# Moving the projection of gate tile 0's first branch from the gate stage into the last attention unit

## Chip, cores and metric

The kernel runs on one NeuronCore (core 0) of a Trainium2 chip. The metric is the device time of one execution in microseconds. Before the change the median of three runs is 918.4 us (917.24 to 919.42). All work is in 32-bit floats; a matmul in full precision is made of three passes over operands split in a high and a low part.

## What is computed

One decoder block on `x` of 1024 positions by 1024 channels. What matters here, cut from the reference:

```
h = rms_norm(x, g_pre)
proj = einsum('bsd,dn->bsn', h, w_in)
qa, ka, va, fa, za, qb, kb, vb, zb, gates = split(proj)
ya = fox_attention(qa, ka, va, log_sigmoid(fa + b_forget)) * silu(za)
yb = rms_norm(diff_attention(rope(qb), rope(kb), vb)) * silu(zb)
gate_a, gate_b = split(sigmoid(gates), 2)          # 1024 channels each
merged = gate_a * (ya @ w_branch[0]) + gate_b * (yb @ w_branch[1])
out = x + rms_norm(merged @ w_out, g_post)
```

The gates are thus a projection of `h` by 2048 columns of `w_in` (from column `GT` = 4104) followed by a sigmoid. They depend on nothing that the attention computes.

## The kernel before, in words

Everything is kept channel-major: a tile is 128 channels by 1024 positions, worked in two chunks `c` of 512 positions. `hT[part][kh][sh]` holds the normalised input, part 0 the high and part 1 the low part; all eight tiles stay in SBUF until the gate stage ends.

Stages in order:

1. Normalise and transpose `x`, project the values (L197), and write combinations of `h` to DRAM (`t_d`, four of them, 2 MB each).
2. Attention: eight units `u` (0 to 3 differential, 4 to 7 forgetting). A unit's work is a list of `groups`; a group is two blocks of 128 query rows: `row` makes logits on TensorE (L432, L433; `s_row`), VectorE adds the bias and takes the maximum (L434), ScalarE the exponential (L440), VectorE the reciprocal (L557), GpSimd the scaling (L558). Then `av` transposes the weights (L461), splits them on ScalarE and VectorE (L464, L465), multiplies by the values (L485) and evacuates (L567, L568), and SyncE stores them (L571). A group's `av` is traced after the rows of the next group (`pend`).
3. Between groups stand projections that depend on no attention result, as work to fill TensorE: the next unit's q and k, the z tiles (`z_tasks`, through `spill_tasks`: `load_w`, `project` at L278, copy at L373, store to DRAM at L374) and sums of squares. In unit 7 the list `fill` holds only the four chunks of z tiles 6 and 7, placed after its groups 0, 1, 2 and 4 (counted from 0). Unit 7 has eight groups, from the longest rows to the shortest; the last two have rows of at most 256 positions.
4. The gate stage. `h_load` (L818) reads the `t_d` combinations back into eight tiles `T`, 1 MB each, in the SBUF that attention used. `gates_plain(0)` projects gate tile 0 directly: for branch 0 and 1 a weight load (`load_w`: DMA at L260, high part on ScalarE at L264, low part on GpSimd at L268) and two chunks of 24 matmuls (L278), each followed by a sigmoid from PSUM and a store to `g_d` (L797, L798). Gate tiles 1 to 7 go through `gates_pair`, which makes a 2x2 block product in seven products `m` of 12 matmuls (L735): the weight combinations on GpSimd (L699), their split (L686, L687), sums on VectorE (L728), sigmoid and store by `gate_out`. Products 1, 2 and 3 read `hT`; 4, 5, 6 and 7 read `T`. For tiles 1 to 6 the order is `GATE` = (1, 2, 4, 6, 5, 7, 3).
5. `y_load` (L782) and `y_work` bring the attention results back beside the gate products; then the branch products (L869), `merge`, and the output product with its norm.

What sets the order: the program is traced by Python loops, and a planner orders each engine's instructions by simulated time; among the instructions that are ready it takes the one traced first. On the chip each engine then runs its own list in order. All DMAs here (but one) are issued by SyncE in its list's order, and an issue that has to wait holds those behind it. Weights share pool slots: two each of `wraw` (raw), `whi` and `wlo`; the split left operands `a_g` of `gates_pair` rotate over `whi`, `wlo` and a third pair, `wop`. `pj` is a PSUM pool of two banks for the fill projections; `tmp` has ten 128x512 tiles for gates and z.

The context `tc.issue_after(ins)` makes the matmuls traced in it stand behind `ins` in TensorE's list; it adds no wait.

Of the kernel before, what the change touches and what calls it, by code (L numbers as in the profile page):

```python
# [9 lines left out]
F32 = mybir.dt.float32  # L10
# [6 lines left out]
P = 128  # L17
S = 1024
D = 1024
KT = D // P  # L20
NB = S // P
CH = 512
# [8 lines left out]
FING = (0,)  # L31
YORD = ((), ((4, 0), (4, 1)), ((5, 0), (5, 1), (6, 0)), ((6, 1), (7, 0), (7, 1)),
        ((0, 0), (0, 1), (1, 0)), ((1, 1), (2, 0), (2, 1)), ((3, 0), (3, 1)), ())
ZFILL = ((0,), (1,), (), (2,), (3,), (4,), (5,), (6, 7))
BIG = 3.0e38
EPS = 1e-6
# [3 lines left out]
QA, KA_, VA, ZA, QB, KB_, VB, ZB, GT = 0, 512, 1024, 1544, 2056, 2568, 3080, 3592, 4104  # L40
# [7 lines left out]
def tile_hybrid_block(  # L48
# [18 lines left out]
    nc = tc.nc  # L67
# [37 lines left out]
    cum_d = dram.tile([8, S], F32, name="cum_d")  # L105
    y_d = [dram.tile([P, S], F32, name=f"y_d{t}") for t in range(8)]
    g_d = [[dram.tile([P, S], F32, name=f"g_d{d}_{b}") for b in range(2)] for d in range(KT)]
    ss_d = dram.tile([4, S], F32, name="ss_d")
    rs_d = dram.tile([4, S], F32, name="rs_d")
    z_d = [dram.tile([P, S], F32, name=f"z_d{t}") for t in range(8)]  # L110
# [172 lines left out]
    with ExitStack() as st:  # L283
# [19 lines left out]
        def unit_proj(u):  # L303

            diff = u < 4
            t = u if diff else u - 4
            qc, kc = (QB, KB_) if diff else (QA, KA_)
            T = {}
            for n in ("TA", "TB", "KA", "KB"):
                T[n] = qk.tile([P, S], F32R, tag=n, name=f"{n}{u}")  # L310

            def rope(ps, c, nm):
                sl = slice(c * CH, (c + 1) * CH)
                raw = stg.tile([P, CH], F32, tag="raw", name=f"raw{nm}", bufs=4)
                nc.scalar.copy(raw, ps)
                sw = stg.tile([P, CH], F32, tag="sw", name=f"sw{nm}")
                for b in range(4):
                    o = b ^ 1
                    nc.sync.dma_start(sw[b * 32:(b + 1) * 32, :], raw[o * 32:(o + 1) * 32, :])
                rot = stg.tile([P, CH], F32, tag="raw", name=f"rot{nm}", bufs=4)  # L320
                nc.vector.tensor_tensor(rot, ps, cosT[:, sl], op=ALU.mult)
                nc.gpsimd.tensor_tensor(sw, sw, sinT[:, sl], op=ALU.mult)
                nc.vector.tensor_tensor(rot, rot, sw, op=ALU.add)
                return rot

            def stack(A, B, src, sl):

                nc.scalar.copy(A[UPR, sl], src[UPR])
                nc.vector.tensor_tensor(A[DNR, sl], src[UPR], A[UPR, sl], op=ALU.subtract)
                nc.scalar.copy(B[DNR, sl], src[DNR])  # L330
                nc.vector.tensor_tensor(B[UPR, sl], src[DNR], B[DNR, sl], op=ALU.subtract)  # L331

            def q_chunk(wt, c):
                sl = slice(c * CH, (c + 1) * CH)
                ps = pj.tile([P, CH], F32, tag="pj", name=f"pq{u}_{c}")
                project(ps, wt, c)
                src = rope(ps, c, f"q{u}_{c}") if diff else ps
                stack(T["TA"], T["TB"], src, sl)

            def k_chunk(wt, c):  # L340
                sl = slice(c * CH, (c + 1) * CH)
                ps = pj.tile([P, CH], F32, tag="pj", name=f"pk{u}_{c}")
                project(ps, wt, c)
                src = rope(ps, c, f"k{u}_{c}") if diff else ps
                stack(T["KA"], T["KB"], src, sl)

            box = {}

            def mk(kind, c, c0):
                def run():  # L350
                    if kind not in box:
                        box[kind] = load_w(f"{kind}{u}", w_cols(c0))
                    (q_chunk if kind == "q" else k_chunk)(box[kind], c)
                return run

            tasks = [mk("k", 0, kc + t * P), mk("q", 0, qc + t * P),
                     mk("k", 1, kc + t * P), mk("q", 1, qc + t * P)]
            return T, tasks
# [57 lines left out]
                    vload.pop(0)()  # L416
            return t

        lastx, vload = [None], []

        def s_row(T, m, i, X, bias, boff, nm, le=None):

            A, B = (T["TA"], T["KA"]) if m == 0 else (T["TB"], T["KB"])
            n = (i + 1) * P
            qs = slice(i * P, (i + 1) * P)
            xs = slice(i % 2 * P, (i % 2 + 1) * P)
            pr = pp.tile([P, S], F32, tag="P", name=f"P{nm}_{m}_{i}")
            mx = small.tile([P, 2], F32, tag="mx", name=f"mx{nm}_{m}_{i}", bufs=8)
            pcs = pieces(i)
            for j, (a, b) in enumerate(pcs):  # L430
                ps = sps.tile([P, CH], F32, tag="S", name=f"S{nm}_{m}_{i}_{j}")[:, 0:b - a]
                nc.tensor.matmul(ps, lhsT=A[:, qs], rhs=B[:, a:b], start=True, stop=False)  # L432
                nc.tensor.matmul(ps, lhsT=X[:, xs], rhs=B[:, a:b], start=False, stop=True)  # L433
                nc.vector.tensor_tensor_reduce(  # L434
                    out=pr[:, a:b], in0=ps, in1=bias[:, boff + a:boff + b], scale=-0.125,
                    scalar=BIG if j == 0 else mx[:, j - 1:j], op0=ALU.add, op1=ALU.min,
                    accum_out=mx[:, j:j + 1])
            if le is None:
                le = small.tile([P, 1], F32, tag="l", name=f"l{nm}_{m}_{i}", bufs=8)
            nc.scalar.activation(pr[:, 0:n], pr[:, 0:n], AF.Exp,  # L440
                                 bias=mx[:, len(pcs) - 1:len(pcs)], scale=-1.0, accum_out=le)
            return pr, le
# [156 lines left out]
        def forget_sums():  # L599
# [27 lines left out]
            nc.vector.tensor_scalar(cum, cum, -8.0, None, op0=ALU.mult)  # L627
            nc.sync.dma_start(cum_d, cum)

        T, tasks = unit_proj(0)  # L630
        for tk in tasks:
            tk()
# [2 lines left out]
        for u in range(8):  # L635
            load, load_v, groups = nxt or unit_attn(u, T)
            nxt = None
            if u == 0:
                vload.append(load_v)
            if u == 1:  # L640
                forget_sums()
            load()
            fill = []
            if u + 1 < 8:
                T, tasks = unit_proj(u + 1)
                fill += tasks
            for t in ZFILL[u]:
                fill += z_tasks(t)
            for t in SFILL[u]:
                fill += [lambda t=t, c=c: sum_squares(t, c) for c in range(2)]  # L650
                fill.append(lambda t=t: subln_scales(t))
            total = sum(s[0] for s in groups)
            done, nf = 0, 0
            for n, (wgt, rws, prd) in enumerate(groups):
                if n == len(groups) // 2 and u < 7:
                    nxt = unit_attn(u + 1, T)
                    vload.append(nxt[1])
                for r in rws:
                    r()
                if pend:  # L660
                    pend()
                pend = prd
                done += wgt
                while nf < len(fill) and nf < len(fill) * done / total:
                    fill[nf]()
                    nf += 1
        pend()

    bigs.close()
# [126 lines left out]
    def gate_out(d, br, c, g, src):  # L796
        nc.scalar.activation(g, src, AF.Sigmoid)  # L797
        nc.sync.dma_start(g_d[d][br][:, c * CH:(c + 1) * CH], g)  # L798

    def gates_plain(d):  # L800
        for br in range(2):
            wt = load_w(f"g{br}_{d}", w_cols(GT + br * D + d * P), True, True)
            for c in range(2):
                ps = xps.tile([P, CH], F32, tag="x", name=f"pg{d}_{br}_{c}")
                project(ps, wt, c)
                gate_out(d, br, c, tmp.tile([P, CH], F32, tag="t", name=f"g{d}_{br}_{c}"), ps)
# [14 lines left out]
    def gates_pair(d, order):  # L821
        raw = []
        for br in range(2):
            r = wpool.tile([P, KT, P], F32, tag="wraw", name=f"raw{d}_{br}")
            nc.sync.dma_start(r, w_cols(GT + br * D + d * P))
            raw.append(r)
        left = left_operands(f"g{d}", raw[0][:, 0:4], raw[0][:, 4:8], raw[1][:, 0:4], raw[1][:, 4:8])
        run_all(wino(f"g{d}", left, h_ops, order,
                     *(lambda t, br=br, c=c: gate_out(d, br, c, t, t)
                       for br in range(2) for c in range(2))))  # L830
# [2 lines left out]
    GATE = (1, 2, 4, 6, 5, 7, 3)  # L833
    h_load()
    gates_plain(0)
    for t in (4, 5, 6, 7, 0, 1, 2, 3):
        y_load(t)
    for d in range(1, KT):
        gates_pair(d, GATE if d < KT - 1 else (7, 5, 6, 4, 1, 2, 3))
        for t, c in YORD[d]:  # L840
            y_work(t, c)
    tst.close()
# [218 lines left out]
```

## Time and profile before

| | us |
|---|---|
| median of three runs | 918.4 |
| the profiled execution | 922.06 |
| its span, first to last instruction | 920.2 |
| TensorE busy | 887.9 (96%) |
| VectorE busy | 606.7 (66%) |
| GpSimd busy | 469.7 (51%) |
| ScalarE busy | 440.4 (48%) |
| gate stage: first matmul of `gates_plain(0)` | 585.39 |

How to read it: times in the views count from the first instruction's start. PE is TensorE's matmul, PEld its weight load, DVE VectorE, ACT ScalarE, POOL GpSimd, SP SyncE. Matmuls are pipelined, so the duration of one (0.39 us for 512 columns) is longer than the distance between the starts of two. A row of windows has for each engine the busy us with the number of instructions in brackets, then the granted clock, the share of the DMA engines and GB/s. A bracket at the end of a timeline row, such as [0.72 <-DVE plf L465], is the idle time before it and what ended it.

### The profile page before, as it was taken

The numbers are of one execution on the slowest core, as the hardware profiler recorded it, in microseconds if no ns is written. First come the engines' busy times: TensorE is split into PE (matmuls) and PEld (weight loads), VectorE is DVE, ScalarE is ACT, GpSimd is POOL, SyncE is SP. The second block draws the span as 40 slices with busy tenths as digits, with TensorE's granted clock in tenths as the row PEclk, the third lists the DMA queues.
The fourth block names the chain that finished last, engine by engine and source line by source line (L and its number), as shares of the span: only waits on it lengthen the run. The fifth ranks groups of instructions, "written<-read, shape, count | busy, mean of one in ns | idle before, by whom it ended". The sixth has DMA issues, their size and how long they took to land. (4 is left out here: it accounts for less than half of the span.)

```text
span 920.2 us, 13659 instructions
## 1 busy us (share of the span) xinstructions
PE 887.9 (96%) x4600; PEld 747.4 (81%) x4600; DVE 606.7 (66%) x1123; ACT 440.4 (48%) x877; POOL 469.7 (51%) x439
## 2 busy tenths in 40 slices
PE   7999999899999999999999999999999999999995
PEld 5899978788887888888888887788888878887874
DVE  6756546878668664467648547416778783549896
ACT  3433225566657675365546648524443461313442
POOL 7325324545545456254434446317676436787851
PEclk9999999999999999999999999999999999999998
DMA  9556737434336350432523331596555497300352
GB/s 315 188 176 256 259 90 197 123 79 123 107 77 172 75 178 18 138 92 72 167 69 97 117 109 54 220 399 207 172 176 169 154 342 258 88 28 25 101 173 91
DMA packets 121416, 136.95 MB, mean 149 GB/s; under 512 B 10225, under 2 KB 88049, under 8 KB 120322
## 3 DMA queue, kind: packets, MB, share of 16 engines
q1 hardware_dynamic: 121202, 135.82, 47.0%
q8 instruction: 36, 0.59, 0.3%
q14 instruction: 34, 0.28, 0.1%
q10 hardware_dynamic: 144, 0.26, 0.1%
HBM read 85.65 MB, written 37.81 MB: 134 GB/s over the span
## 5 line engine op out<-in xcount | busy, mean ns | idle before, releaser
L197 PE MATMUL pv<-wvhi,hT 128*128 128x264 f32 (+2 forms) x384 | 88.9, 324 | 0.4 <-DVE hT L183 0.4
L278 PE MATMUL pz<-hT,hi_z 128*128 128x512 f32 x256 | 83.3, 397 | 0.2 <-ACT sq L390 0.2
L278 PE MATMUL pk<-hT,hi_k 128*128 128x512 f32 x256 | 82.3, 395 | 0.9 <-DVE KB L331 0.9
L278 PE MATMUL pq<-hT,hi_q 128*128 128x512 f32 x256 | 82.9, 399 | 0.0
L735 PE MATMUL x_o<-wo_op,a_o 128*128 128x512 f32 x336 | 78.3, 393 | 1.6 <-ACT a_o L686 1.1
L869 PE MATMUL pb<-yT,hi_br 128*128 128x512 f32 x256 | 78.4, 389 | 0.0
L735 PE MATMUL x_g<-T,a_g 128*128 128x512 f32 x336 | 78.1, 391 | 0.0
L735 PEld LDWEIGHTS x_o<-wo_op,a_o 128*128 128x128 f32 x336 | 62.8, 188 | 17.0 <-ACT a_o L686 2.0
L735 PEld LDWEIGHTS x_g<-T,a_g 128*128 128x128 f32 x336 | 63.1, 188 | 13.9
L197 PEld LDWEIGHTS pv<-wvhi,hT 128*128 128x128 f32 x384 | 64.3, 190 | 6.1 <-DVE hT L183 0.7
L440 ACT ACTIVATE Pd<-Pd,mxd 128x128 f32<-128x128 f32 (+7 forms) x64 | 49.6, 775 | 35.4 <-DVE mxd L434 35.1
L553 POOL TENSOR_TENSOR cb<-cb,trim 128x128 f32<-128x128 f32 x64 | 30.1, 475 | 65.9 <-DVE mxf L434 44.7
L527 POOL TENSOR_SCALAR Pd<-Pd,l,nlam 128x128 f32<-128x128 f32 (+7 forms) x32 | 29.2, 912 | 67.0 <-DVE l L526 60.7
L197 PE MATMUL pv<-wvlo,hT 128*128 128x512 f32 (+2 forms) x192 | 61.9, 325 | 0.4 <-DVE wvlo L153 0.4
L558 POOL TENSOR_SCALAR Pf<-Pf,lf 128x1024 f32<-128x1024 f32 (+3 forms) x64 | 47.7, 750 | 27.7 <-DVE lf L557 24.6
L465 DVE TENSOR_TENSOR plf<-ptf,phf 128x512 fp32r<-128x512 f32 (+1 forms) x80 | 50.0, 635 | 18.0 <-ACT phf L464 17.1
L440 ACT ACTIVATE Pf<-Pf,mxf 128x1024 f32<-128x1024 f32 (+3 forms) x64 | 49.8, 778 | 20.6 <-DVE mxf L434 19.9
L735 PE MATMUL x_g<-hT,a_g 128*128 128x512 f32 x252 | 59.0, 391 | 0.0
L869 PEld LDWEIGHTS pb<-yT,hi_br 128*128 128x128 f32 x256 | 48.1, 188 | 9.9
L278 PEld LDWEIGHTS pq<-hT,hi_q 128*128 128x128 f32 x256 | 48.3, 191 | 9.5
L735 PEld LDWEIGHTS x_g<-hT,a_g 128*128 128x128 f32 x252 | 47.3, 188 | 10.4
L278 PEld LDWEIGHTS pk<-hT,hi_k 128*128 128x128 f32 x256 | 47.2, 188 | 10.3 <-DVE KB L331 1.5
(248 smaller groups left out, 2382.8 us busy)
## 6 DMA issues: line engine op xcount, KB each, us to landing
t_d<-t SPq DMA_DIRECT2D x16, 512.0 KB, 4.8
T<-t_d SPq DMA_DIRECT2D x8, 1024.0 KB, 17.9
raw<-in_w_in_dram SPq DMA_DIRECT2D x14, 512.0 KB, 5.2
vb_d<-vbs SPq DMA_DIRECT2D x8, 512.0 KB, 3.7
va_d<-vas SPq DMA_DIRECT2D x8, 512.0 KB, 3.0
raw_k<-in_w_in_dram SPq DMA_DIRECT2D x8, 512.0 KB, 5.1
raw_q<-in_w_in_dram SPq DMA_DIRECT2D x8, 512.0 KB, 4.1
V<-vb_d SPq DMA_DIRECT2D x4, 1024.0 KB
```

Of the source, the lines that this page charges most:

```text
L197: nc.tensor.matmul(ps[n], lhsT=hT[hp][k // 4][i // 4][:, k % 4, hs], rhs=wt[k][:, a:b], start=first, stop=(k == KT - 1 and hp == 1))
L278: nc.tensor.matmul(ps, lhsT=a[:, k, :], rhs=hT[h][k // 4][c][:, k % 4, :], start=(k == 0 and a is hi and h == 0), stop=(k == KT - 1 and a ...
L440: nc.scalar.activation(pr[:, 0:n], pr[:, 0:n], AF.Exp, bias=mx[:, len(pcs) - 1:len(pcs)], scale=-1.0, accum_out=le)
L465: nc.vector.tensor_tensor(pl[:, 0:n], pt[:, 0:n], ph[:, 0:n], op=ALU.subtract)
L527: nc.gpsimd.tensor_scalar(p2[:, 0:n], p2[:, 0:n], l2, nlam, op0=ALU.mult, op1=ALU.mult)
L553: nc.gpsimd.tensor_tensor(diag, diag, trim, op=ALU.add)
L558: nc.gpsimd.tensor_scalar(p1[:, 0:n], p1[:, 0:n], l1, 1.0, op0=ALU.mult, op1=ALU.mult)
L735: nc.tensor.matmul(x[m], lhsT=a[:, ai, k, :], rhs=right[m][bi][k], start=(k == 0 and n == 0), stop=(k == 3 and n == 2))
L869: nc.tensor.matmul(ps, lhsT=a[:, kk, :], rhs=yT[g][h][:, k % 2, sl], start=(k == 0 and a is hi and h == 0), stop=(k == 3 and a is lo))
```

## The change

Branch 0 of gate tile 0 becomes two fill tasks of unit 7, made by `spill_tasks` as the z tiles are. The first chunk is traced after group 5 and the second after group 7 (the last), each with its matmuls behind the last logits matmul traced so far. Its raw result is copied from PSUM and stored to the new DRAM tile `gl_d`. In the gate stage `gates_plain(0)` projects only branch 1; then the two chunks are loaded from `gl_d` into `tmp` tiles, put through the sigmoid and stored to `g_d`. Gate tile 1 takes its products in the order (1, 2, 3, 4, 6, 5, 7).

```
+GFILL = (5, 7)
...
+    gl_d = dram.tile([P, S], F32, name="gl_d")
...
-        lastx, vload = [None], []
+        lastx, vload, lasts = [None], [], [None]
...
-                nc.tensor.matmul(ps, lhsT=X[:, xs], rhs=B[:, a:b], start=False, stop=True)
+                lasts[0] = nc.tensor.matmul(
+                    ps, lhsT=X[:, xs], rhs=B[:, a:b], start=False, stop=True).ins
...
+        gate = spill_tasks("gl", GT, gl_d)
         T, tasks = unit_proj(0)
...
                 while nf < len(fill) and nf < len(fill) * done / total:
                     fill[nf]()
                     nf += 1
+                if u == 7 and n in GFILL:
+                    with tc.issue_after(lasts[0]):
+                        gate[GFILL.index(n)]()
         pend()
...
     def gates_plain(d):
-        for br in range(2):
+        for br in (1,):
...
     gates_plain(0)
+    for c in range(2):
+        g = tmp.tile([P, CH], F32, tag="t", name=f"g0_0_{c}")
+        nc.sync.dma_start(g, gl_d[:, c * CH:(c + 1) * CH])
+        gate_out(0, 0, c, g, g)
     for t in (4, 5, 6, 7, 0, 1, 2, 3):
         y_load(t)
     for d in range(1, KT):
-        gates_pair(d, GATE if d < KT - 1 else (7, 5, 6, 4, 1, 2, 3))
+        gates_pair(d, (1, 2, 3, 4, 6, 5, 7) if d == 1 else GATE if d < KT - 1 else (7, 5, 6, 4, 1, 2, 3))
```

## The prediction

> **What bounds the kernel now.** I read the page first, then stretches around the end of attention, then that stretch's matmuls by form and in order of time.
>
> ```profile
> PE 887.9 (96%) x4600; PEld 747.4 (81%) x4600; DVE 606.7 (66%) x1123; ACT 440.4 (48%) x877; POOL 469.7 (51%) x439
> PE   7999999899999999999999999999999999999995
> ```
>
> TensorE is nearly always busy, so a gain must come from a place where it isn't. The slice of the page that holds the end of attention shows nothing: it still says 9. But a busy matmul is not one at its peak, so I look closer. The next view is the table of stretches (columns: PE, PEld, DVE, ACT, POOL busy, clock, DMA share, GB/s).
>
> ```profile
> 553.90:569.07 15.17, 14.55 (x100) 12.45 (x99) 12.87 (x40) 12.20 (x24) 10.50 (x13) 1.00 0.25 71
> 585.39:607.20 21.81, 21.81 (x98) 18.06 (x98) 2.54 (x4) 5.09 (x8) 6.10 (x5) 1.00 0.98 397
> 569.07:585.39 16.32, 13.62 (x98) 11.30 (x98) 12.71 (x40) 13.00 (x35) 7.91 (x15) 1.00 0.06 21
> ```
>
> The last row is the tail of attention, from the logits of the 6th group of unit 7 to the first matmul of the gate stage. In it TensorE shows 13.62 of 16.32 us busy, VectorE 12.71 and ScalarE 13.00: three engines hand work to one another and none is full. The middle row is the stretch that the change halves: gate tile 0, 96 wide matmuls in 21.81 us, 0.227 us apart, without a gap. The clock is 1.00 in all.
>
> How much of the tail is free? The matmuls in it by form, then some in order of time:
>
> ```profile
> L461 PE MATMUL ptf<-ident,Pf 128*128 128x128 f32 x38 | 6.2, 280 | 1.6 <-DVE plf L465 1.5
> L485 PE MATMUL ypf<-plf,V 128*128 128x256 f32 x19 | 5.6, 311 | 0.4 <-DVE plf L465 0.4
> L485 PE MATMUL ypf<-phf,V 128*128 128x256 f32 x18 | 5.1, 314 | 0.7 <-ACT phf L464 0.3 <-DVE ys L568 0.2
> L485 PE MATMUL ypf<-plf,V 128*128 128x128 f32 x7 | 1.9, 275 | 0.0
> L485 PE MATMUL ypf<-phf,V 128*128 128x128 f32 x7 | 1.5, 221 | 0.0
> ...
> 572.92 0.28 PE L485 MATMUL ypf<-plf,V 128*128 128x256 f32 x1
> 573.04 0.28 PE L485 MATMUL ypf<-phf,V 128*128 128x256 f32 x1
> 573.16 0.60 PE L461 MATMUL ptf<-ident,Pf 128*128 128x128 f32 x4
> 573.51 0.36 PE L485 MATMUL ypf<-plf,V 128*128 128x256 f32 x1
> 573.71 0.22 PE L485 MATMUL ypf<-phf,V 128*128 128x128 f32 x1
> 573.77 0.27 PE L485 MATMUL ypf<-plf,V 128*128 128x128 f32 x1
> ```
>
> A product of 256 columns shows 0.31 us, but the next starts 0.12 later; one of 128 columns takes 0.06 in the line; four transposes 0.35. So the tail's work is 38 transposes x 0.088 = 3.3, 37 x 0.117 = 4.3, 14 x 0.06 = 0.8, and nine logits matmuls (the 98 less these), at most 0.9: together 9.3 us. 16.3 - 9.3 = 7.0 us of TensorE's time are free there, far more than the 2.7 that its busy column leaves.
>
> **What moves.** Of the 96 matmuls, 48 leave the gate stage: 48 x 0.227 = 10.9 us less there, where nothing else limits it. They go where the edges allow: chunk 0 behind the logits of the 6th group, chunk 1 behind the very last logits.
>
> ```profile
> 568.89 0.34 PE L433 MATMUL Sf<-KB,X1f 128*128 128x384 f32 x1
> 577.71 0.28 PE L433 MATMUL Sf<-KB,X1f 128*128 128x128 f32 x1
> 584.40 0.39 PE L485 MATMUL ypf<-phf,V 128*128 128x256 f32 x1 [0.32 <-ACT phf L464]
> 585.00 0.39 PE L485 MATMUL ypf<-plf,V 128*128 128x256 f32 x1 [0.21 <-DVE plf L465]
> ```
>
> The free 7.0 us lie on both sides of 577.71, and each side takes 5.45 us of projection, so neither chunk finds room for all of itself. Together they need 20.2 us (9.3 + 10.9) against 16.3: the tail grows by at least 3.9.
>
> On top: the last product chain has gaps (0.32 and 0.21 in the rows) behind which no projection may be left, 0.5. Two new ScalarE copies of 128x512 from PSUM stand in the tail; the z tiles' copies are the same operation.
>
> ```profile
> L373 ACT COPY sz<-pz x16: 564/587/606, 178.6 to 554.8; 128x512 f32<-128x512 f32 x16
> L266 POOL TENSOR_SCALAR hi_z<-raw_z x8: 1047/1054/1492, 160.2 to 510.5; 128x1024 fp32r<-128x1024 f32 x8
> L268 DVE TENSOR_TENSOR lo_z<-raw_z,hi_z x8: 1220/1226/1627, 162.1 to 512.1; 128x1024 fp32r<-128x1024 f32 x8
> L264 ACT CAST hi_g<-raw_g x2: 1047/1054/1060, 536.3 to 553.8; 128x1024 fp32r<-128x1024 f32 x2
> L268 POOL TENSOR_TENSOR lo_g<-raw_g,hi_g x2: 2396/2400/2404, 538.4 to 555.4; 128x1024 fp32r<-128x1024 f32 x2
> ```
>
> Two copies are 1.2 us if both delay the chain and nothing if TensorE has projections to do meanwhile; ScalarE is free for 3.3 of 16.3 us and the tail gets longer, so I take 0.6. What stands behind such a copy in ScalarE's list are the split `phf` and the copy `yt`, for which transposes and products wait. So the tail goes to 9.3 + 10.9 + 0.5 + 0.6 = 21.3 us, 5.0 more, for 10.9 less behind it: a gain of 5.9.
>
> The weights: the high part goes from ScalarE to GpSimd (1.05 us on both), the low part from GpSimd (2.40) to VectorE (1.23). Both old operations of the first tile lie at 536 to 541, 30 us ahead of the tail, where z projections keep TensorE at work; I cost this at nothing, at most the 1.2 us of VectorE if the planner puts it into the tail. The number of sigmoids, weight DMAs and gate stores is the same. New are two stores and two loads of 256 KB.
>
> **DMA behind the tail.** Here the cover could go. SyncE's issues and the DMA share:
>
> ```profile
> T<-t_d SPq DMA_DIRECT2D x8, 1024.0 KB, 17.9
> ...
> 584.74 1.36 SPq L818 DMA_DIRECT2D T<-t_d  x3
> 587.05 3.56 SPq L818 DMA_DIRECT2D T<-t_d  x5
> 593.96 0.38 SPq L825 DMA_DIRECT2D raw<-in_w_in_dram  x1
> 596.44 7.42 SPq L798 DMA_DIRECT2D g_d<-g  x1
> 603.91 3.77 SPq L782 DMA_DIRECT2D yd<-y_d  x4
> ...
> 594.00:600.00 6.00, 6.00 (x29) 4.95 (x27) 0.69 (x1) 1.62 (x3) 1.29 (x1) 1.00 1.01 421
> ```
>
> `T` waits for the SBUF of attention, so it cannot start before the tail's end. It is 8 x 1.05 = 8.4 MB; at 421 GB/s that is 20 us, with the slow start some 22 after the last product (my estimate from these rows). Tile 1 needed its first `T` product at 21.8 + 24 x 0.227 = 27.3 us into the gate stage. With 10.9 gone and product 3 drawn forward (36 x 0.227 = 8.2) it needs `T` 4 at 19.1, `T` 6 at 21.8, 5 at 24.5 and 7 at 27.3. They are loaded in the order 4, 6, 5, 7, so they are there at about 7, 12, 17 and 22: 5 us to spare at the least, also with 0.5 MB of new stores (1.2 us) ahead.
>
> Tile 2's weights have less room:
>
> ```profile
> 619.06 0.62 ACT L686 CAST a_g<-raw 128x512 fp32r<-128x512 f32 x1 [2.75 <-DMA raw<-in_w_in_dram]
> 620.34 1.30 POOL L687 TENSOR_TENSOR a_g<-raw,a_g 128x512 fp32r<-128x512 f32 x1
> 631.99 11.13 PE L735 MATMUL x_g<-T,a_g 128*128 128x512 f32 x48
> ```
>
> The second weight tile landed at 619.06, 33.7 us into the stage, and its first operand was ready at 621.64, 10.3 before TensorE came to it (631.99). With 10.9 less that room is gone: 0.6 us short if it lands as late again, nothing if its slot frees earlier. I take 0.5.
>
> Sum: 5.9 - 0.5 = 5.4 us gained. The profiled execution took 922.06 us for a span of 920.2, 3.7 more than the median of the runs; from 918.4 it is 913.0. About 0.2% (1.8 us) is what a measurement of this kernel can tell from no change.
>
> **Rivals.** *The tail is fuller than I read it.* PEld stands at 11.30 of 16.32 us there, against 18.06 of 21.81 in the dense stretch. If narrow matmuls needed their weight loads' slots as the wide ones do, only 16.32 - 11.30 x 21.81 / 18.06 = 2.7 us would be free; less 0.6 for the copies the gain is 2.1: 916.3. [...] The trace disagrees: products start 0.12 apart though each has its own load. Chance 0.12.
>
> *The projection delays the chain instead of filling it.* Chunk 0 is traced ahead of the last rows and of two `av`, so the planner prefers it. If each chunk ran as a block with VectorE and ScalarE waiting for what stands behind, up to 10.9 us would be given back: no change, 918.4. Against it, logits wait for VectorE, not the reverse:
>
> ```profile
> 569.79 0.37 PE L432 MATMUL Sf<-KA,TA 128*128 128x256 f32 x1
> ...
> 576.50 0.41 DVE L434 CUSTOM_DVE_ANT_0 Pf<-Sf,cb 128x256 f32<-128x256 f32 x1
> ```
>
> Those of the 7th group were made 6.7 us before VectorE read them, so a block of 5.45 us delays little. Chance 0.10.
>
> *ScalarE waits for the reloaded chunks.* The loads from `gl_d` stand behind `T` in SyncE's list and in the queue; a store of `g` was held 7.42 us at issue by 603.9. Behind a sigmoid that waits for such a load stand ScalarE's casts for tile 1's `T` products, if the planner expects the load early. The first such product is due at 19.1; two sigmoids, a cast and GpSimd's subtraction are 0.6 + 0.6 + 0.6 + 1.3 = 3.1, so from a landing at 16.0 us on TensorE waits, and from 21.4 the gain is gone. If the load is issued only when that store was through (18.5) and lands 9.5 later (the median for the stores of `g`), at 28, TensorE loses 12 us: 6.6 slower, 925.0.
>
> ```profile
> g_d<-g SPq DMA_DIRECT2D x4, 256.0 KB, 9.5
> 591.13 0.60 ACT L797 ACTIVATE g<-pg 128x512 f32<-128x512 f32 x1 [0.22 <-PE pg L278]
> ```
>
> For it: DMA share 1.01. Against it: the planner put the `yd` loads behind `raw` and a store of `g`, as if it knew that the queue is full. Chance 0.16, nearly all slower.
>
> **The numbers.** My forecast has 0.62, at 913.0, with its own range 911 to 915 (all 7.0 us filled, to both copies and a VectorE split on the chain). Faster by over 0.2%: 0.62 and two thirds of the first rival, 0.70. Within 0.2%: the rest of that and the second, 0.14. Slower: 0.16. The range 910.5 to 919.5 takes in both rivals near no change; the low end adds 0.9 us for the restarts between groups, which I left in the work.
>
> **What would show it.** Right: projection matmuls between 569 and the tail's end, that tail 20 to 22 us long, no TensorE idle time from then to tile 2, and 48 matmuls before tile 1's products. Wrong: a tail of 25 us or more (rivals one and two), or TensorE idle in tile 1 with ScalarE at a sigmoid that waits for DMA (rival three), or tile 2 late by more than 1 us.

## The result

The changed kernel takes 930.1 us (median of 4 runs, 929.07 to 933.27) against 918.1 for the kernel before (4 runs, 917.24 to 919.42): ratio 1.012 [1.010, 1.015]. It is slower by 12 us where a gain of 5.4 was forecast. The profiled execution took 929.75 us for a span of 928.0. Two executions of later kernels ran at a granted clock of 0.56 and 0.66 (1465.5 and 1463.9 us); they are in no median here, and the kernel whose profiled execution was one of them was run a second time.

The profile of before in the first part has its first z projection 1.7 us later than a second profile of the same kernel, taken beside the experiments (919.07 us, span 917.3). The second is nearer to the median, so the traces are compared with it from here on. Up to the last z projection, where no work was changed, the profiled executions differ by up to 5.5 us (the two of the kernel before reach it at 553.6 and 551.4 us), so the stages below are counted from there.

### The profile page after: what moved, and what is told of

Read it like the earlier page. It is cut to its first block, busy times and chain, and to the rows that moved or that the text cites. A ratio compares the mean times of both kernels' runs of the same rounds, so it can differ in the third digit from the quotient of the medians.

```text
span 928.0 us, 13662 instructions
## 1 busy us (share of the span) xinstructions
PE 889.1 (96%) x4600; PEld 747.1 (81%) x4600; DVE 610.8 (66%) x1124; ACT 439.4 (47%) x878; POOL 472.0 (51%) x439
## 5 line engine op out<-in xcount | busy, mean ns | idle before, releaser
L742 PE MATMUL x_g<-T,a_g 128*128 128x512 f32 x336 | 80.6, 399 | 5.4 <-ACT a_g L693 4.7
L443 ACT ACTIVATE Pd<-Pd,mxd 128x128 f32<-128x128 f32 (+7 forms) x64 | 49.6, 775 | 35.5 <-DVE mxd L437 35.1
```

The lines of the kernel that those rows point to most:

```text
L443: nc.scalar.activation(pr[:, 0:n], pr[:, 0:n], AF.Exp, bias=mx[:, len(pcs) - 1:len(pcs)], scale=-1.0, accum_out=le)
L742: nc.tensor.matmul(x[m], lhsT=a[:, ai, k, :], rhs=right[m][bi][k], start=(k == 0 and n == 0), stop=(k == 3 and n == 2))
```

## The profile after

Busy time and, in 40 slices, TensorE's busy tenths and its granted clock (the page of the changed kernel):

```profile
PE 889.1 (96%) x4600; PEld 747.1 (81%) x4600; DVE 610.8 (66%) x1124; ACT 439.4 (47%) x878; POOL 472.0 (51%) x439
PE   6999999999999999999999999997999989999995
PEclk9999999999999999999999999998999999999998
```

One slice that had a 9 for TensorE, the 28th (626 to 650 us), now has a 7, with an 8 in the clock: a hole of some us. The 33rd, where the branch stage starts, has an 8. The rest is too coarse. By stretches (columns as in the first part), first the second profile of before: the tail of attention and gate tile 0.

```profile
566.81:583.12 16.31, 13.64 (x99) 11.33 (x98) 12.71 (x40) 13.01 (x35) 7.89 (x15) 1.00 0.06 21
583.12:604.95 21.83, 21.83 (x98) 18.08 (x98) 2.55 (x4) 5.12 (x9) 6.13 (x5) 1.00 0.99 398
```

Then the changed kernel: tail, gate tile 0, from tile 1 to the middle of tile 2, and the hole in two parts.

```profile
566.77:591.63 24.86, 23.10 (x147) 20.07 (x146) 13.92 (x41) 14.63 (x38) 10.38 (x17) 1.00 0.10 36
591.63:602.57 10.94, 10.94 (x50) 9.06 (x50) 2.13 (x3) 3.41 (x6) 2.46 (x2) 1.00 0.97 374
602.57:627.10 24.53, 24.53 (x108) 20.08 (x107) 7.01 (x10) 6.98 (x12) 3.09 (x2) 1.00 1.03 405
627.10:632.00 4.90, 0.41 (x2) 0.00 (x0) 0.69 (x1) 2.36 (x4) 0.42 (x1) 0.83 1.09 373
632.00:637.00 5.00, 4.08 (x9) 2.78 (x10) 1.64 (x2) 1.39 (x3) 5.00 (x5) 0.50 0.72 278
```

Gate tile 0 is shorter by 21.83 - 10.94 = 10.9, as forecast. The tail is longer by 24.86 - 16.31 = 8.55, not 5.0. And TensorE stands still for almost 5 us in gate tile 2, then works at half the clock (0.50) for 5 more. The same from the starts of single matmuls (us; the last matmul is the end):

| | last z projection to gate tile 0 | gate tile 0 to tile 1 | 1 to 2 | 2 to 3 | 3 to branch stage | branch stage to output product | from there to the end |
|---|---|---|---|---|---|---|---|
| before | 31.7 | 21.8 | 19.2 | 19.2 | 96.2 | 87.5 | 79.1 |
| after | 39.8 | 10.9 | 19.2 | 27.1 | 99.7 | 88.9 | 79.1 |

So the sum is +8.1 in the tail, -10.9 in tile 0, +7.9 in tile 2, and +3.5 and +1.4 later, where nothing was changed: +10.0. The medians differ by 12.0; the other 2 us lie in no stage of these two executions, which were themselves 10.7 us apart.

What happens in the tail (in brackets the idle time before an instruction and what ended it). In the timeline of before, a product of an `av` starts 0.18 us behind the logits of the 6th group (566.65):

```profile
566.83 0.32 PE L485 MATMUL ypf<-plf,V 128*128 128x256 f32 x1
```

In the timeline of the changed kernel:

```profile
566.60 0.34 PE L435 MATMUL Sf<-KB,X1f 128*128 128x384 f32 x1
566.77 0.62 PE L280 MATMUL pgl<-hT,hi_gl 128*128 128x512 f32 x2
...
570.87 0.39 PE L280 MATMUL pgl<-hT,hi_gl 128*128 128x512 f32 x1
571.10 0.28 PE L488 MATMUL ypf<-plf,V 128*128 128x256 f32 x1
...
571.59 0.37 ACT L570 COPY yt<-ypf 64x256 f32<-64x256 f32 x1 [3.52 <-PE ypf L488]
571.99 0.42 DVE L571 TENSOR_TENSOR ys<-ypf,yt 64x256 f32<-64x256 f32 x1 [3.73 <-ACT yt L570]
...
576.92 0.55 PE L464 MATMUL ptf<-ident,Pf 128*128 128x128 f32 x3 [0.47 <-DVE plf L468]
583.31 0.37 ACT L570 COPY yt<-ypf 64x256 f32<-64x256 f32 x1 [3.09 <-PE ypf L488]
588.41 0.39 PE L488 MATMUL ypf<-phf,V 128*128 128x256 f32 x1 [0.77 <-DVE ys L571]
```

From 566.77 to 571.10 stand 19 projection matmuls in one block, ahead of the last three products of an `av`; the same product now starts 4.5 us behind these logits. ScalarE is idle for 3.52 us and VectorE for 3.73, waiting for these products (VectorE through ScalarE's copy); a second block, of 15, does it again (3.09). Once the blocks are through, TensorE waits for the others as before (0.47, 0.77).

The hole in tile 2. Before, tile 2's second weight load went out 23.6 us into the gate stage:

```profile
606.76 0.38 SPq L825 DMA_DIRECT2D raw<-in_w_in_dram  x1
```

In the timeline of the changed kernel (SyncE's issues first):

```profile
598.88 0.38 SPq L832 DMA_DIRECT2D raw<-in_w_in_dram  x1
599.36 11.02 SPq L805 DMA_DIRECT2D g_d<-g  x1
610.43 1.68 SPq L789 DMA_DIRECT2D yd<-y_d  x3
612.21 3.94 SPq L789 DMA_DIRECT2D yf<-y_d  x4
...
622.78 0.38 SPq L832 DMA_DIRECT2D raw<-in_w_in_dram  x1
...
602.55 0.62 ACT L693 CAST a_g<-raw 128x512 fp32r<-128x512 f32 x1 [4.62 <-PE pg L280]
628.54 1.30 ACT L804 ACTIVATE g<-g 128x512 f32<-128x512 f32 x2 [2.69 <-DMA g<-gl_d]
631.53 0.62 ACT L693 CAST a_g<-raw 128x512 fp32r<-128x512 f32 x1 [0.16 <-DMA raw<-in_w_in_dram]
631.58 1.27 POOL L706 TENSOR_TENSOR S_g<-raw 128x512 f32<-128x512 f32 x1 [12.68 <-DMA raw<-in_w_in_dram]
632.20 1.22 PE L742 MATMUL x_g<-T,a_g 128*128 128x512 f32 x2 [4.69 <-ACT a_g L693]
634.14 12.21 PE L742 MATMUL x_g<-T,a_g 128*128 128x512 f32 x46 [0.72 <-POOL a_g L694]
```

Tile 2's first weight tile goes out at 598.88; the second only at 622.78, behind the eight `y` loads and the two reloads, and lands at 631.5: 31.2 and 39.9 us into the stage. GpSimd had waited 12.68 us for it. ScalarE also waited for a reloaded chunk (2.69), but was through with both at 629.8, 1.7 us before the weights came. Why the second load stands so late: it needs the slot of tile 1's second weight tile. In tile 1's new order that tile is read last by the operand for product 4, whose cast at 602.55 had to wait until the last projection freed a weight slot.

## The experiments

Three theories stand behind the later runs (the expectations of the first four spell out their own). **A**: in the tail TensorE, VectorE and ScalarE form a chain; a projection is free only where TensorE would have waited at that very point, and a block elsewhere delays all of them. Tile 2's loss comes from the order of tile 1 through the late weight load. **P**: the prediction's terms (7.0 us free, whatever is put there). **E**: the later stages need the 10.9 us as cover for transfers that start with attention's end. "Old order" below means tile 1's products in the order of the kernel before:

```
-        gates_pair(d, (1, 2, 3, 4, 6, 5, 7) if d == 1 else GATE if d < KT - 1 else ...)
+        gates_pair(d, GATE if d < KT - 1 else ...)
```

All runs together; the middle columns are us between starts of matmuls in the trace, and the last is the ratio to runs of the kernel before on the same chip, with its interval. The us between starts come from one execution each; the two of the kernel before differ by 0.7 us from gate tile 0 to the end (323.8 and 323.1).

| | projections in the tail | last z to gate tile 0 | gate tile 0 to the end | median us | ratio |
|---|---|---|---|---|---|
| before, second profile | 0 | 31.7 | 323.1 | 919.07 (one run) | |
| the change | 48 in blocks | 39.8 | 325.0 | 930.1 | 1.012 [1.010, 1.015] |
| change, old order | 48 in blocks | 39.9 | 316.6 | 922.9 | 1.0043 [1.0026, 1.0059] |
| change, y loads behind | 48 in blocks | 39.8 | 319.1 | 924.6 | 1.0062 [1.0045, 1.0079] |
| change, late reload | 48 in blocks | 39.8 | 322.1 | 926.9 | 1.0089 [1.0068, 1.0110] |
| tail extra, all behind | 48 in blocks | 39.7 | 322.7 | 927.6 | 1.0099 [1.0077, 1.0121] |
| branch 0 left out | 0 | 31.6 | 312.2 | 908.9 | 0.9886 [0.9867, 0.9906] |
| before, new order | 0 | 31.8 | 324.4 | 920.1 | 1.0022 [1.0007, 1.0036] |
| pieces, old order | 48 in threes | (z moved) | 313.4 | 920.3 | 1.0023 [1.0006, 1.0040] |
| no reload, old order | 48 in blocks | 39.9 | 318.1 | 922.2 | 1.0049 [1.0030, 1.0067] |
| half, block | 24 in a block | 35.5 | 318.5 | 918.2 | 1.0010 [0.9995, 1.0026] |
| half, seven steps | 24 in 7 steps | 32.8 | 327.7 | 925.1 | 1.0071 [1.0059, 1.0083] |
| half, steps, weights kept | 24 in 7 steps | 32.9 | 318.3 | 915.5 | 0.9970 [0.9959, 0.9981] |
| all in seven steps | 48 in 7 steps | 38.4 | 313.3 | 916.1 | 0.9975 [0.9964, 0.9986] |

**Before, once more.** Unchanged, for a second profile.

> The kernel before, profiled once more. The first profile of it was 3.9 us above the median of its runs, the profile of the changed kernel was not. If that was one execution's own delay, this profile gives a span near 916 and shows where the 4 us lay; if profiling always costs it, the span is 920 again. The tail of attention should again end near 585.4 and TensorE should be without a gap from there to the branch products.

919.07 us; it is the reference of the stage columns.

**The change with tile 1's old order** (the diff above).

> The changed kernel with gate tile 1's products in the old order. Theory A (the new order keeps tile 1's second weight tile in use until its fourth product's operand is made, so the load of tile 2's second weight tile is listed behind 4 MB of y loads): that load is now listed right behind tile 2's first one, lands before TensorE needs it, the 8 us lost in tile 2 are gone, and the 4.7 us gained in the tail remain: 913 to 914. Theory C (the reload of the two chunks delays it): as slow as the change, 928 to 930. Theory D (the DMA queue is simply too full when TensorE comes 11 us sooner): part of the loss stays, 917 to 925.

922.9 us. Tile 2 takes 19.95 us instead of 27.1, and TensorE waits for none of its weights: without the new order there is no hole. But the kernel is still slower than before, in theory D's span and not in theory A's: its tail is as long as the changed kernel's, and behind it it loses 4.4 us against the 312.2 that the gate stage should leave (below). The timeline shows a wait for the first operand of tile 3 and one at the start of the branch stage:

```profile
641.58 0.73 PE L742 MATMUL x_g<-hT,a_g 128*128 128x512 f32 x2 [0.54 <-ACT a_g L693]
739.95 1.20 PE L880 MATMUL pb<-yT,hi_br 128*128 128x512 f32 x4 [1.19 <-ACT hi_br L266]
```

ScalarE's list explains the first. Its row for the cast that tile 3 waits for, and the sigmoid listed ahead of that cast:

```profile
639.86 0.63 ACT L804 ACTIVATE c_g<-c_g 128x512 f32<-128x512 f32 x1 [4.58 <-DVE c_g L735]
640.92 0.60 ACT L693 CAST a_g<-raw 128x512 fp32r<-128x512 f32 x1
```

ScalarE was idle for 4.58 us up to that sigmoid, though GpSimd was at work on tile 3's weights from 638.72. In the last kernel below, all 48 in the seven steps, the same casts are listed ahead of the sigmoid (its timeline), and tile 3 loses nothing:

```profile
636.40 1.13 ACT L720 CAST a_g<-raw 128x512 fp32r<-128x512 f32 x2
```

**The y loads behind tile 2's weights**, new order kept:

```
+            raw2 = raws(2)                       # tile 2's two weight loads
+            with tc.issue_after(lastr[0]):
+                for t in (4, 5, 6, 7, 0, 1, 2, 3):
+                    y_load(t)
```

> The changed kernel with the eight y loads listed behind the load of tile 2's second weight tile; tile 1's order stays the new one. Theory A in the narrow sense (the slot is freed too late): the load still waits for the slot until 13 us into the gate stage and for a full queue, and tile 2 still loses some us: 918 to 926. Theory B (the 4 MB of y loads ahead of it are what makes it late): it lands some 10 us sooner and tile 2 loses nothing: 913 to 915. Theory C (the reload, which stays ahead of it): 928 to 930.

924.6 us. The second load goes out 20.5 us into the stage, and tile 2's own products run without a wait: the hole is gone, as theory B said, but not the time that B forecast. The 21.5 us from tile 2 to tile 3 end with a wait of 2.10 us for tile 3's first operand, whose cast stands behind a sigmoid as above; tile 3 then takes 21.0 us at a clock that fell to 0.53 for its first 3.5 us (last section).

**The reload traced after gate tile 3**, new order kept (the loop over `gl_d` moves into `if d == 3`).

> The changed kernel with the reload of the two chunks, their sigmoid and store traced after gate tile 3, the rest as it is. Theories A and B: the load of tile 2's second weight tile still stands behind the y loads and comes at most 2 us sooner: 926 to 929. Theory C (the reload holds SyncE's list and ScalarE): tile 2 loses little, 914 to 917.

926.9 us, as theories A and B said. Tile 2 still takes 25.7 us: the reload was worth 1.4 of the 7.9. TensorE waits at the same instruction (timeline of this kernel), with no reloaded chunk on ScalarE ahead of it:

```profile
629.67 0.73 PE L742 MATMUL x_g<-T,a_g 128*128 128x512 f32 x2 [3.23 <-ACT a_g L693]
```

**The tail's projections as an extra**: they are made and stored, nothing reads them, and the gate stage has both branches.

```
-        for br in (1,):
+        for br in range(2):
...
-    for c in range(2):
-        g = tmp.tile([P, CH], F32, tag="t", name=f"g0_0_{c}")
-        nc.sync.dma_start(g, gl_d[:, c * CH:(c + 1) * CH])
-        gate_out(0, 0, c, g, g)
```

> The two chunks are still projected in attention's tail and stored, but nothing reads them: the gate stage projects both branches of tile 0 as before, and tile 1 runs its products in the old order. The 48 matmuls of the tail are extra work whose result is unused, so this prices the tail alone, with the old cover behind it. Theory A (two blocks of projections delay the chain): the tail grows by 8.5 us as in the two changed kernels so far, gate stage and branch stage lose nothing, 918.4 + 8.5 = 927 (926 to 928). Theory P (the prediction's terms: 7.0 us are free, the tail grows by 5.0): 923.4 (922.5 to 924.5). If the branch stage again takes 88.7 us and not 87.3, that loss belongs to the tail and not to the missing cover.

927.6 us, in theory A's span. The tail grows by 8.0 us, and nothing is lost behind it (322.7 against 323.1). The interval of the ratio, 7.1 to 11.1 us, takes in these 7.6.

**Branch 0 of tile 0 left out** (in the kernel before, `gates_plain` runs for branch 1 alone and stores its sigmoid twice).

> The kernel before without the first branch's projection of gate tile 0: the sigmoid of the second branch is stored for both, so that one of the two gates of tile 0 is left out. Tail of attention and order of the gate stage are as before; only the 48 matmuls (10.9 us) are gone. Theory P (nothing else limits the gate stage): 918.4 - 10.9 = 907.5 (907 to 908.5). Theory E (transfers and the chain behind them start with the end of attention and need those 10.9 us as cover): 2.5 to 5 us of it are given back in tiles 2 and 3 and at the start and in the course of the branch stage, 910 to 912.5, with the branch stage at 88.7 and not 87.3 us.

908.9 us, 0.4 above theory P's span and below E's. From gate tile 0 to the end it is 312.2 us, 10.9 less than before: the gate stage gives back nothing when its cover goes. Theory E falls in this form; the prediction's term of 10.9 us was right.

**The kernel before with tile 1's new order** (that one line of the change).

> The kernel before with one line of the change: tile 1's products in the order 1, 2, 3, 4, 6, 5, 7. Theory A2 (the new order lets tile 2's second weight load go out about 7 us later, and the 10.9 us taken from the gate stage are why TensorE then waits for it): here TensorE reaches tile 2 10.9 us later, the load lands at about 40 us into the stage and its last operand is ready at 41 to 42.5, tile 2's third product begins at 41.3 + 11 = 52 - no loss: 918.4 (917.9 to 919.2). Rival (the order costs by itself): tile 2 late by 2 us or more, 920.5 or slower.

920.1 us, a little over the expected span. Tile 2's second weight load is late here too, and the timeline shows why it costs nothing at that place: GpSimd waits for it until 40.1 us into the gate stage, as in the changed kernel, but TensorE comes to the first `T` product only 6.5 us after that, without a wait.

```profile
616.05 0.38 SPq L825 DMA_DIRECT2D raw<-in_w_in_dram  x1
625.73 1.30 POOL L699 TENSOR_TENSOR S_g<-raw 128x512 f32<-128x512 f32 x1 [5.44 <-DMA raw<-in_w_in_dram]
632.24 11.18 PE L735 MATMUL x_g<-T,a_g 128*128 128x512 f32 x48
```

So the order needs the cover that the change takes away: neither part makes the hole alone. By its ratio the order costs some 2 us all the same (0.6 to 3.3); the trace shows 1.2 of them from gate tile 0 on, in the branch stage.

**Pieces**: old order, the 48 matmuls in 16 steps of three, one behind each group of transposes or products, from the fifth group on.

```
+                if steps:
+                    with tc.issue_after(last.ins):
+                        steps.pop(0)()
```

> The change with tile 1's old order, and the 48 projection matmuls of the tail split into 16 steps of three, each behind a group of transposes or products of the tail, so that the longest run of them is six instead of 19. Theory A (the blocks delay the chain of transposes, splits and products): from the last z projection to the first gate matmul 39.9 us shrink to 36.5 to 38 (31.7 before), and the time falls by as much below the 922.9 of the kernel with the old order alone: 919.5 to 921.5. Rival (the tail simply has more work than was read, blocks or not): 39.5 us or more, 922.5 to 923.5.

920.3 us lies in theory A's range, but not for its reason. The planner put the last z projections between the steps, so that the expected distance can't be read. From the first z projection to gate tile 0 it is 430.7 us, against 420.2 before and 429.2 with blocks: of 10.9 us of projections next to nothing was absorbed (the distance grew by 10.5). Waits stand where the z projections had been, the longest 0.63 us at 553.58 of its timeline; that they account for the whole was not shown. What this kernel gained over the blocks it gained behind the tail (313.4 against 316.6).

**No reload**, old order: the projected chunks stay in DRAM, branch 1's sigmoid is stored for both.

> The kernel with tile 1's old order, where the projected chunks stay in DRAM: they are not reloaded, and the second branch's sigmoid is stored for both, so that one of the two gates of tile 0 is left out. Theory R (the 4 us that the kernel with the old order loses behind the tail belong to the two loads and two late sigmoids): from the first gate matmul to the end 323.5 us, as in the kernel without the projection; 918.4 + 8.5 - 10.9 = 916 (915.5 to 917.5). Theory E (the loss belongs to the longer tail, since what stands behind attention starts later): 326 to 328 us, 919.5 to 922.

922.2 us, and 318.1 us behind the tail (329.3 to the end of the span, as the expectation counts): slower than both theories said. The reload is not what costs there.

**Half the projection, in a block** (old order, `GFILL = (5,)`, the second chunk in the gate stage) and **in seven steps**. The waits of TensorE in before's timeline give the places:

```
+HOOKS = (("S", 0, 1, 3), ("t", 0, 2, 2, 2), ("S", 0, 0, 2), ("S", 1, 1, 5), ("t", 0, 1, 1, 4),
+         ("t", 1, 1, 0, 4), ("t", 0, 0, 0, 4))    # S logits, t transposes: behind which, how many
```

> The same half of the projection, placed as in the change: 19 matmuls in one block behind the logits of the 6th group and 5 a little later. Same amount of work as in the seven steps, so it tells place from amount. Theory A: from the last z projection to the first gate matmul 36 us (half of the growth of 8.5 that two chunks gave), 2 to 3 us more than with the seven steps; 917.5 to 919. Theory P (7 us of free time are there for whatever comes): 32.5 us, 914.

> Only the first chunk (24 matmuls, 5.45 us) is projected in the tail, in seven steps of two to five, each put straight behind the instruction after which TensorE waited in the kernel before; the second chunk goes back to the gate stage, tile 1 has its old order. Theory A (the tail is a chain; a projection is free only where TensorE would have waited at that point, and elsewhere it delays the chain): the seven waits together are worth about 4 us, so from the last z projection to the first gate matmul 31.7 us become 32.5 to 34, the gate stage is 5.45 us shorter, and the time falls to 914 to 916.5. Rival (TensorE's free time in the tail can't be used, wherever the steps stand): 36 us or more, no gain, 918 to 919.5.

The same 24 matmuls, the same old order: in a block the tail grows by 3.7 us, in the seven steps by 1.0. The amount is equal, so the 2.7 us between them come from the place. Stretches from the last z projection to gate tile 0, of the block:

```profile
552.15:587.60 35.45, 32.73 (x220) 28.08 (x219) 25.52 (x79) 27.38 (x62) 21.07 (x30) 1.00 0.22 62
```

and of the seven steps:

```profile
551.45:584.21 32.76, 31.45 (x221) 27.77 (x219) 25.87 (x79) 27.18 (x61) 19.61 (x28) 1.00 0.18 51
```

The kernel with the block took 918.2 us, as theory A said. But the one with the steps took 925.1, slower than both its theories. It lost 8 us in tile 1 and 2 more behind it (its timeline):

```profile
592.42 0.38 SPq L854 DMA_DIRECT2D raw<-in_w_in_dram  x1
609.42 0.62 ACT L715 CAST a_g<-raw 128x512 fp32r<-128x512 f32 x1 [1.75 <-DMA raw<-in_w_in_dram]
610.10 1.20 PE L764 MATMUL x_g<-T,a_g 128*128 128x512 f32 x2 [3.87 <-ACT a_g L715]
```

With the weights of this branch loaded and split twice, and held until the last step, tile 1's second weight tile got its slot late and went out at 592.42, behind the 8 MB of `T`; with the block it had gone out at 578.60, ahead of them.

**Seven steps, weights kept** for the second chunk:

```
-            wt = load_w(f"g{br}_{d}", w_cols(GT + br * D + d * P), True, True)
+            wt = load_w(f"g{br}_{d}", w_cols(GT + br * D + d * P), True, True) if br else marks["w"]
...
+                if u == 7 and n == 5:
+                    marks["w"] = load_w("gl", w_cols(GT), True, True)
```

The kept weights are also loaded two groups earlier and split on ScalarE and GpSimd, not on GpSimd and VectorE, so that this run does not tell these three apart.

> The seven steps again, with the weights of the tail's chunk kept for the gate stage's second chunk, so that no second copy of them is loaded and split and tile 1's second weight load goes out ahead of the T loads, as in the kernel before. Theory A with the weights as the cause of the 10 us lost behind the tail: from the last z projection to the first gate matmul 32.8 us as with the seven steps, from there to the end 317.7 us (the kernel before's 323.1 less 24 x 0.227), no wait of TensorE in tile 1: 913.5 to 915. Rival (the steps themselves, or the later end of the tail, cost what was lost in tile 1): 920 or slower, with TensorE idle in tile 1 again.

> The half version with its weights kept, once more, for a profile at the full clock. Theory A: from the last z projection to the first gate matmul 32.8 us, from there to the end 317.7 us, TensorE without a wait of over 0.3 us between the first gate matmul and tile 4; time 914 to 916. Rival: the 10 us of tile 1's wait were gone only in part, 319 us or more from the first gate matmul.

915.5 us (12 runs, ratio 0.9964 [0.9950, 0.9978]; 9 more runs, the row of the table). In the profile of the second series it is 32.87 us from the last z projection to gate tile 0, tile 1's wait is gone, and the stages behind took 318.3 where 317.7 was expected. One of the steps, of five matmuls, shows how it works. In before's timeline the transposes behind these logits wait:

```profile
572.23 0.28 PE L433 MATMUL Sf<-KB,X1f 128*128 128x256 f32 x1
573.21 0.55 PE L461 MATMUL ptf<-ident,Pf 128*128 128x128 f32 x3 [0.70 <-DVE plf L465]
```

In this kernel's timeline five projection matmuls stand there instead, and the transposes start 1.27 us behind the logits where they had started 0.98 behind them:

```profile
573.23 0.28 PE L436 MATMUL Sf<-KB,X1f 128*128 128x256 f32 x1
573.34 0.39 PE L648 MATMUL pgl<-hT,hi_gl 128*128 128x512 f32 x1
573.57 0.40 PE L648 MATMUL pgl<-hT,lo_gl 128*128 128x512 f32 x1
573.81 0.62 PE L648 MATMUL pgl<-hT,hi_gl 128*128 128x512 f32 x2
574.27 0.40 PE L648 MATMUL pgl<-hT,lo_gl 128*128 128x512 f32 x1
574.50 0.49 PE L465 MATMUL ptf<-ident,Pf 128*128 128x128 f32 x3
```

**All 48 in the seven steps**, old order, twice as many in each.

> Both chunks in the tail, as in the change, but in the seven places of the half version, with twice as many matmuls in each (48); tile 1 in its old order. Theory A (the waits of TensorE at these seven places are worth about 4 us and no more): the second 24 matmuls delay the chain by their whole 5.45 us, so from the last z projection to the first gate matmul 32.8 + 5.45 = 38.2 us (37.7 to 38.7; blocks gave 39.9), and the second half brings nothing: 914 to 916 if the stages behind lose nothing, 918 to 921 if they lose the 4 us that they lost behind the other full versions. Theory P (7.0 us are free): 36 us or less.

916.1 us, with 1.1 us lost behind the tail. From the last z projection to gate tile 0:

```profile
553.12:591.48 38.36, 36.95 (x245) 32.29 (x243) 26.58 (x80) 28.07 (x64) 19.16 (x29) 1.00 0.17 51
```

The second half cost its whole 5.45 us (38.36 - 32.87 = 5.5). What is absorbed is the projection's time less the growth: 10.9 - 6.6 = 4.3 us for 48 matmuls, 5.45 - 1.1 = 4.3 for 24, and 10.9 - 8.1 = 2.8 for the change's blocks (5.45 - 3.7 = 1.7 for the block of the half). So the place counts up to some 4 us, and beyond that every projection is paid in full.

## Why the prediction was wrong

The forecast gain was 10.9 - 5.0 - 0.5 = 5.4 us; the traces have 10.9 - 8.1 - 7.9 - 4.9 = -10.0. Two terms were mis-sized, the tail and tile 2's weights, and one was missing.

- *"7.0 us of TensorE's time are free there", so that the tail grows by 5.0.* It grew by 8.1 to 8.5. The 7.0 us are a sum of many waits, and what they are worth depends on the place: the same 24 matmuls made the tail 3.7 us longer in a block and 1.0 longer in seven steps ahead of instructions that had waited. Taken start by start with the prediction's own costs, the second profile of before has 7.1 us in its tail: 4.6 at ten places of 0.23 to 0.86 us, and the other 2.5 in pieces of at most 0.11, shorter than one projection matmul (0.227). In blocks 2.8 us were absorbed, at seven places chosen from the waits 4.3. I had rejected the rival "the projection delays the chain" by looking at the logits alone (6.7 us early); what the blocks delayed were products, and ScalarE and VectorE behind them. The rival was right in its mechanism and wrong in its size: of the forecast gain of 5.9 us it takes 3.1 to 3.5, not all.
- *The rival "the tail is fuller than I read it"*: by the weight loads 2.7 us would have been free. The blocks' 2.8 look like it, but the same matmuls at other places got 4.3, so it isn't the bound. By these runs its 2.7 us were nearer than my 7.0 from the distances of starts, and still too low.
- *"Tile 2's weights ... I take 0.5."* This is the step that failed by most: 7.9 us, with the half clock in it. I kept the landing time of before (33.7 us into the stage) and asked only whether TensorE would come earlier. The new order of tile 1, which I read as a help (it draws product 3 forward ahead of `T`), also moves back the point at which tile 1's second weight tile is let go. Its slot carries tile 2's second load, which went out at 31.2 us into the stage and landed at 39.9. In the planner's list that put the load behind the `y` loads; listed ahead of them, it went out at 20.5 us and tile 2 did not wait. The new order alone cost some 2 us and made no hole, and the missing cover alone cost nothing; only together do they make TensorE wait.
- *The rival "ScalarE waits for the reloaded chunks"* did happen (2.69 us), but the weights came later still: 1.4 us at most, with the reload moved. Its price of 12 us counted on the reload being the last to come.
- *48 x 0.227 = 10.9 us out of the gate stage, with nothing else limiting it*: right, 10.9 in gate tile 0 and 10.9 to the end with the branch left out.
- *The `T` loads have 5 us to spare*: no product of tile 1 waited in the changed kernel. Right. The weights' split at nothing: right as well.
- Not in the sum: 3.5 us between tile 3 and the branch stage and 1.4 in it. Losses there stand in all versions with both blocks and a shortened gate stage (from gate tile 0 on 4.4 with the old order, 5.9 without the reload). They are not in the kernel without the projection (0), nor in the one with an unshortened stage (-0.4), and only 1.1 with all 48 in steps or in threes. So it isn't the missing cover alone, not the reload, and not the longer tail alone. What also differs is the order in which the planner then lists loads on SyncE and casts on ScalarE. For the wait at tile 3 the traces show this order (the cast behind a sigmoid, above); for the rest, most of it around the start of the branch stage, it is left by exclusion, and it wasn't tried by itself.

## What to carry to other kernels

In this tail TensorE's free time was worth 4.3 us at instructions that wait, against 7.0 by the sum, and the second 24 matmuls at the same places cost their whole 5.45 us. So list the waits with their places, put pieces of their length there, and count the rest as full cost. Before moving work out of a stage, ask of each load in it when its slot is let go, and not when it landed before. The version that does both (half of the projection, in seven steps, weights kept) is 0.3% faster than the kernel before.

## What the hardware showed

TensorE's granted clock fell to about half at both waits below. In the changed kernel, with a wait of 4.69 us, it was 0.50 from 630.38, still in the wait, to 637.21. In the kernel with the `y` loads behind, it was 0.53 behind a wait of 2.10 us (one row of its timeline, then stretches of it; the second has the end of the matmuls ahead of the wait in it):

```profile
643.51 5.76 PE L742 MATMUL x_g<-hT,a_g 128*128 128x512 f32 x17 [2.10 <-ACT a_g L693]
...
641.03:643.50 2.47, 0.38 (x2) 0.00 (x0) 1.90 (x4) 2.47 (x6) 0.00 (x0) 1.00 0.65 243
643.50:647.00 3.50, 3.49 (x9) 2.68 (x10) 0.69 (x1) 1.40 (x3) 2.94 (x3) 0.53 0.23 80
647.00:650.00 3.00, 3.00 (x14) 2.48 (x13) 1.11 (x1) 1.26 (x3) 3.00 (x3) 0.98 0.00 0
```

The 3.5 us after it run at 0.53, with the matmuls 0.43 us apart instead of 0.227. At 647 the clock is back. Nine matmuls in 3.5 us instead of 2.0 make the wait of 2.10 us cost some 3.6 (an estimate from these rows). Behind the wait of 1.19 us with the old order (739.95 above) no such fall shows: from 743.40 to 748.64 of that timeline 23 matmuls start 0.228 us apart.

One DMA issue was held for 11.02 us on SyncE (the store at 599.36 above), while the DMA engines moved 427 GB/s in these 11.02 us; the next issue came at 610.43, and all that was listed behind it, weights too, waited with it.
